# A two-layer decoder trunk: the norms' factors moved from ScalarE and VectorE to a power on GpSimd

## The chip, the cores and the metric

The kernel runs on one core of a Trainium2 chip. A core has a matrix engine (PE), with its weight loads shown apart (PEld), a vector engine (DVE), a scalar engine (ACT) and GpSimd (POOL). Each executes its own queue in order, and they meet at semaphores. DMA transfers are issued from the queues of SyncE (SP), ACT and POOL. The metric is the device time of one launch in microseconds; lower is better. A time given for a kernel is the median of several runs, and beside it stands one profiled execution, whose trace is read.

## The reference

The input x has 1024 rows of 1024 floats, the memory mem has 256 rows of 1024. Two layers follow one another, and everything is in float32:

```python
def rmsnorm(x, g):
    y = x * lax.rsqrt(jnp.mean(x * x, axis=-1, keepdims=True) + EPS)   # EPS = 1e-6
    return y * g

mem_n = rmsnorm(mem, mem_norm_g)
for i in range(2):
    hn = rmsnorm(x, attn_norm_g[i])
    mix, q_cross = mla_mixer(hn, ...) if i == 0 else swa_mixer(hn, ...)
    cross = memory_cross_attention(q_cross, mem_n, w_mem_kv[i])
    x = x + jnp.concatenate([mix, cross], -1) @ w_o[i]
    x = x + squared_relu_mlp(rmsnorm(x, mlp_norm_g[i]), w_up[i], w_down[i])
return rmsnorm(x, final_norm_g)
```

Layer 0's mixer is multi-head latent attention (12 heads, causal over all rows); inside it two more norms act on the low-rank query part (384 columns) and key-value part (256 columns). Layer 1's mixer is a sliding window of 128 with sinks. The MLP is `relu(h @ w_up)**2 @ w_down`, with 4096 hidden columns.

What the change touches is the factor of each norm, one number for each row: `1 / sqrt(mean(x*x) + EPS)`.

## The kernel before, in words

**Tiling.** Rows lie on the 128 partitions, so x is eight tiles of 128 rows and mem two; a norm's factor is one number in each partition, a 128x1 operand. Matrix products are done in a split of float32 into two parts: ACT copies the rounded part (L99 and L102, the names end in h), DVE subtracts to get the rest (L100 and L103, names in l), and PE does three products for one. So every operand of PE goes through ACT and then DVE. A normed row tile must also be transposed by PE before it can be an operand.

**Order of the work.** The program is written through a framework that takes the program's operations, estimates when each could run, and lays down one in-order queue for each engine, so an instruction's place in its queue depends on what the framework expects of all the others. Nobody wrote the order of the queues by hand, but it is fixed when the kernel is built.

**Stages**, with the times in the profiled execution:
- Head, to 62 us. The memory arrives, is transposed (psTm, L473), split (memTh, memTl) and multiplied by the memory weights (psmk, L342 to L344; the weight's parts are wmh and wml). The first tiles of x are scaled by their factors (fa, L209), transposed (psT_a, L216), split (xhls) and multiplied by the input weights wih and wil (psin). DVE computes the tables of the rotary embedding there too (rt, L244 to L293). The copies ktok and mrs belong to the memory's keys: mrs is the factor of a memory tile.
- Layer 0's inputs and attention, to about 500 us.
- Output projection of layer 0 (`wo_phase`, pswo), about 480 to 540 us: each of eight row tiles is added to x (L1294), written to DRAM by two DMAs from POOL's queue (L1303), normed (L1225 to L1231) and transposed (psT_m, L1241; called T_m(0) to T_m(7) here, by their places in the order). The first products of the MLP (psu, psv, L1421 to L1423) stand behind them in PE's queue.
- MLP of layer 0. The products are arranged as a seven-product scheme of block matrices, so that operands are sums and differences that DVE makes. The down projection (class `Down`, psy and psz, L1728 to L1730) adds its result to x (L1681), writes it out from POOL's queue (L1699), norms it (L1700 to L1710) and transposes it (psT_b, L1721; T_b(0) to T_b(7)) for layer 1.
- Layer 1 likewise; its down projection ends with the final norm, whose rows are scaled (L1707, L1712) and written out from the queues of SP and ACT.

**The norms.** There are 50 factors to compute, in two forms.

`rstd_of` (L172 to L181) with `newton` (L183 to L193) serves 18: the two memory tiles (`mem_root`, L477 on), the eight tiles of x (`norm_y`, L206), and the eight tiles in `a_in` (L618), where the query and key-value parts are done together as two columns. ACT squares the row and accumulates the sum (L179), DVE forms mean plus epsilon (L180), ACT takes the root (L187), DVE the reciprocal (L188) and one correcting Newton step (L189 to L192).

The class `Rstd` (L1141 to L1160) serves the other 32: eight in each output projection and eight in each down projection. Squares are accumulated for two halves of a row (`half`, L1150), already scaled to a mean; `get` adds the halves and epsilon on DVE (L1154), takes the root on ACT (L1155), the reciprocal on DVE (L1156), and the correcting step on DVE (L1157 to L1159). Its scratch columns lie in tiles named cosb and sinb, so these names mark the steps in the trace.

A root on ACT needs its function table: where another function ran before, a table load precedes it. At the start one small activation (L518) makes ACT load the table for the root early.

## Time and profile before

| | |
|---|---|
| median of three runs | 2112.05 us (2109.84 to 2112.26) |
| the profiled execution, its own time | 2109.36 us |
| span, first to last instruction | 2107.5 us |
| busy: PE, PEld | 2082.1 us (99%), 1691.0 us (80%) |
| busy: DVE, ACT, POOL | 1476.6 us (70%), 1114.6 us (53%), 147.9 us (7%) |
| mean granted clock of the matrix engine | 0.999 |
| DMA | 292.34 MB, mean 139 GB/s |

How to read it: busy time is the time in which an engine executed something; a matmul's end is modelled, and matmuls are pipelined, so an almost full PE is one that hardly ever lacked an operand. Rows of the timeline give the start, the duration, the engine, the source line, the operation, output and input names and the shape; a bracket at the end gives how long the engine had stood before, and what released it. In the list of waits a row reads: who waited, for whom, and the total, the count and the longest. Line numbers are those of the kernel before, unless said otherwise.

### The profile page before, as it was taken

The numbers are of one execution on the slowest core, as the hardware profiler recorded it, in microseconds if no ns is written. First come the engines' busy times: TensorE is split into PE (matmuls) and PEld (weight loads), VectorE is DVE, ScalarE is ACT, GpSimd is POOL, SyncE is SP. The second block draws the span as 40 slices with busy tenths as digits, with TensorE's granted clock in tenths as the row PEclk, the third lists the DMA queues.
The fourth block names the chain that finished last, engine by engine and source line by source line (L and its number), as shares of the span: only waits on it lengthen the run. The fifth ranks groups of instructions, "written<-read, shape, count | busy, mean of one in ns | idle before, by whom it ended". The sixth has DMA issues, their size and how long they took to land.

```text
span 2107.5 us, 28961 instructions
## 1 busy us (share of the span) xinstructions
PE 2082.1 (99%) x9830; PEld 1691.0 (80%) x9830; DVE 1476.6 (70%) x2929; ACT 1114.6 (53%) x2408; POOL 147.9 (7%) x248
## 2 busy tenths in 40 slices
PE   8999999999999999999999999999999999999998
PEld 7888766678888888888888878778788888888887
DVE  8766677775977776976557535666977776976565
ACT  7554466656755444444445435776755444444453
POOL 1001001010000000000001133420000000000000
PEclk9999999999999999999999999999999999999999
DMA  6202223343355446954433634542345446844342
GB/s 237 79 1 76 63 64 92 91 136 100 112 169 165 152 143 231 321 152 156 136 119 103 153 90 126 140 136 85 111 164 165 159 141 231 318 150 154 119 120 88
DMA packets 180756, 292.34 MB, mean 139 GB/s; under 512 B 16659, under 2 KB 70784, under 8 KB 180608
## 3 DMA queue, kind: packets, MB, share of 16 engines
q1 hardware_dynamic: 174096, 272.07, 41.4%
q0 software_dynamic: 5200, 15.80, 2.1%
q10 hardware_dynamic: 1312, 2.63, 0.4%
q8 instruction: 77, 1.26, 0.3%
q14 instruction: 71, 0.58, 0.1%
HBM read 187.34 MB, written 81.18 MB: 127 GB/s over the span
## 4 chain that ended last, share of the span: by engine, by line
PE 90%; DVE 5%; DMA 2%; ACT 2%; issue 1%; SPq 0%; DVEq 0%; ACTq 0%
PE psy L1730 5%; PE psy L1728 5%; PE psy L1729 5%; PE psu L1421 5%; PE psu L1422 5%; PE psu L1423 5%; PE psz L1728 4%; PE psz L1730 4%; PE psz L1729 4%; PE psv L1422 4%; PE psv L1421 4%; PE psv L1423 4%; PE pso L947 4%; PE pss L917 3%; PE pswo L108 3%; PE pswo L110 3%
## 5 line engine op out<-in xcount | busy, mean ns | idle before, releaser
L927 ACT ACTIVATE p<-pss 128x512 f32<-128x512 f32 (+2 forms) x144 | 68.7, 487 | 69.2 <-DVE pss L925 52.5
L1728 PE MATMUL psy<-g 128*128 128x512 f32 x256 | 99.9, 390 | 0.0
L1729 PE MATMUL psy<-g 128*128 128x512 f32 x256 | 99.6, 389 | 0.0
L1730 PE MATMUL psy<-g 128*128 128x512 f32 x256 | 99.4, 390 | 0.0
L99 ACT ACTIVATE g<-i 128x512 fp32r<-128x512 f32 x79 | 49.7, 629 | 92.5 <-PE psz L1729 46.0
L100 DVE TENSOR_TENSOR g<-i,g 128x512 fp32r<-128x512 f32 x79 | 55.6, 704 | 47.6 <-ACT g L99 47.6
L99 ACT ACTIVATE i<-mr 128x512 fp32r<-128x512 f32 x78 | 47.8, 628 | 74.0 <-PE psy L1729 25.6
L796 DVE TENSOR_REDUCE m<-psx 128x1 f32<-128x1024 f32 (+7 forms) x96 | 72.0, 752 | 20.1 <-PE psx L795 19.7
L99 ACT ACTIVATE uh<-i 128x512 fp32r<-128x512 f32 x66 | 41.7, 631 | 83.9 <-PE psy L1729 39.5
L947 PE MATMUL pso<-p,vf 128*128 128x512 f32 (+2 forms) x192 | 85.4, 527 | 0.6 <-ACT p L927 0.6
L100 DVE TENSOR_TENSOR uh<-i,uh 128x512 fp32r<-128x512 f32 x66 | 45.6, 690 | 46.8 <-ACT uh L99 46.6
L1728 PE MATMUL psz<-g 128*128 128x512 f32 x192 | 74.7, 389 | 0.0
L1729 PE MATMUL psz<-g 128*128 128x512 f32 x192 | 74.7, 389 | 0.0
L1730 PE MATMUL psz<-g 128*128 128x512 f32 x192 | 74.7, 389 | 0.0
L1320 ACT ACTIVATE mr<-mr,gcol 128x256 f32<-128x256 f32 (+1 forms) x160 | 63.9, 475 | 13.5 <-DMA mr<-in_mlp_w_up_dram 13.5
L100 DVE TENSOR_TENSOR i<-mr,i 128x512 fp32r<-128x512 f32 x78 | 53.6, 687 | 21.5 <-ACT i L99 21.5
L917 PE MATMUL pss<-qh,kh 97*128 97x512 f32 (+2 forms) x144 | 67.9, 474 | 0.0
L917 PE MATMUL pss<-ql,kh 97*128 97x512 f32 (+2 forms) x144 | 58.2, 404 | 0.0
L1641 DVE TENSOR_TENSOR mqf<-mqq,mqf 128x512 f32<-128x512 f32 x64 | 43.4, 688 | 20.6 <-DMA mqq<-in_mlp_w_down_dram 20.3
L1730 PEld LDWEIGHTS psy<-g 128*128 128x128 f32 x256 | 48.1, 188 | 10.0
L1729 PEld LDWEIGHTS psy<-g 128*128 128x128 f32 x256 | 48.1, 188 | 9.9
L1728 PEld LDWEIGHTS psy<-g 128*128 128x128 f32 x256 | 48.1, 188 | 9.8
(658 smaller groups left out, 6862.2 us busy)
## 6 DMA issues: line engine op xcount, KB each, us to landing
i<-hd SPq DMA_DIRECT2D x154, 256.0 KB
hd<-uh SPq DMA_DIRECT2D x76, 256.0 KB
hd<-ul SPq DMA_DIRECT2D x76, 256.0 KB
mr<-in_mlp_w_up_dram SPq DMA_DIRECT2D x36, 512.0 KB
hd<-x SPq DMA_DIRECT2D x72, 256.0 KB
mr<-hd SPq DMA_DIRECT2D x70, 256.0 KB
d<-in_mlp_w_up_dram SPq DMA_DIRECT2D x32, 512.0 KB
mqq<-in_mlp_w_down_dram SPq DMA_DIRECT2D x32, 512.0 KB
```

The source lines that it names most:

```text
L99: nc.scalar.activation(hi, src, AF.Copy)
L100: nc.vector.tensor_tensor(lo, src, f32(hi), ALU.subtract)
L796: nc.vector.reduce_max(m8s[h][:, i : i + 1], ps[:, :n], axis=AX, negate=True)
L917: return lambda: nc.tensor.matmul(o, a, b, skip_group_check=True, **kw)
L927: nc.scalar.activation(p[:, c0:], ps, AF.Exp, scale=SC)
L947: mms.append(lambda: nc.tensor.matmul(o, a, b, skip_group_check=True, **kw))
L1421: nc.tensor.matmul(ps, wh[:, k, :], xh[:, k, :], start=p in (1, 2, 5) and k == 0, stop=False, skip_group_check=True)
L1422: nc.tensor.matmul(ps, wh[:, k, :], xl[:, k, :], start=False, stop=False, skip_group_check=True)
L1423: nc.tensor.matmul(ps, wl[:, k, :], xh[:, k, :], start=False, stop=k == 3, skip_group_check=True)
L1728: nc.tensor.matmul(ps, ah[:, j, :], bh, start=p in (1, 5, 2) and k == 0, stop=False, skip_group_check=True)
L1729: nc.tensor.matmul(ps, ah[:, j, :], bl, start=False, stop=False, skip_group_check=True)
L1730: nc.tensor.matmul(ps, al[:, j, :], bh, start=False, stop=k == NP - 1, skip_group_check=True)
```

## The change

Every factor is now one power: (mean of squares + epsilon) to the power −0.5, on POOL. In `rstd_of` the square's scale is the root of 1/n, so that ACT's accumulator holds the mean; POOL adds epsilon and raises to the power. In `get` POOL adds the halves and epsilon and raises to the power. The exponent is a pair of columns filled with −0.5 once at the start. The root, the reciprocal, the Newton steps and the scratch tiles zs are gone, and so is a function that nothing called (`rstd_halves`). The early small activation now asks for a sine, so the table loaded first is another.

```diff
     def rstd_of(pl, src_parts, junk):
...
-        z = pl.tile([P, 2], F32, tag="zs", bufs=4, name=f"zs{small_ct[0]}")
+        rs = pl.tile([P, 2], F32, tag="rs", bufs=4, name=f"rs{small_ct[0]}")
         for i, (ap, n) in enumerate(src_parts):
-            nc.scalar.activation(junk[:, :n], ap, AF.Square, accum_out=ss[:, i : i + 1])
-            nc.vector.tensor_scalar(z[:, i : i + 1], ss[:, i : i + 1], 1.0 / n, EPS, ALU.mult, ALU.add)
-        return newton(pl, ss, z[:, :k], k)
...
+            nc.scalar.activation(junk[:, :n], ap, AF.Square, scale=float(np.float32(n ** -0.5)), accum_out=ss[:, i : i + 1])
+        nc.gpsimd.tensor_scalar(ss[:, :k], ss[:, :k], EPS, None, ALU.add)
+        nc.gpsimd.tensor_tensor(rs[:, :k], ss[:, :k], neg_half[:, :k], ALU.pow)
         return rs
...
     nc.gpsimd.memset(padl, 0.0)
     nc.gpsimd.memset(padr, 0.0)
+    neg_half = padl[:, 32:34]
+    nc.gpsimd.memset(neg_half, -0.5)
...
-    nc.scalar.activation(padl[:, 0:1], eps_t, AF.Sqrt)
+    nc.scalar.activation(padl[:, 0:1], eps_t, AF.Sin)
...
         def get(self):
-            ss, z, rk, t = self.st[:, 0:2], self.st[:, 2:3], self.st[:, 3:4], self.st[:, 4:5]
-            nc.vector.tensor_scalar(z, ss[:, 0:1], ss[:, 1:2], EPS, ALU.add, ALU.add)
-            nc.scalar.activation(t, z, AF.Sqrt)
-            nc.vector.reciprocal(rk, t)
-            nc.vector.scalar_tensor_tensor(t, rk, z, rk, ALU.mult, ALU.mult)
-            nc.vector.tensor_scalar(t, t, -0.5, 1.5, ALU.mult, ALU.add)
-            nc.vector.tensor_tensor(rk, rk, t, ALU.mult)
+            ss, z, rk = self.st[:, 0:2], self.st[:, 2:3], self.st[:, 3:4]
+            nc.gpsimd.tensor_scalar(z, ss[:, 0:1], ss[:, 1:2], EPS, ALU.add, ALU.add)
+            nc.gpsimd.tensor_tensor(rk, z, neg_half[:, 0:1], ALU.pow)
             return rk
```

ACT's queue now holds two table loads in place of seven. Since the framework orders the queues anew, work around the norms moves too. The change's own lines are numbered lower by then: L1154 to L1159 became L1134 and L1135, L180 and L181 are the two POOL steps of `rstd_of`, and L209, L350, L480, L1699, L1721 and L1728 to L1730 are now L187, L330, L460, L1675, L1697 and L1704 to L1706.

The first place is DVE's queue at the very start. There ss, zs and rs are the first memory tile's sum, mean and factor, memTl the rest part of the transposed memory, gcol the gains. Before:

```order
L180 TENSOR_SCALAR zs_233<-ss_232 128x1
L188 RECIPROCAL rs_236<-ss_232 128x1
L189 TENSOR_TENSOR ss_232<-rs_236 128x1
L190 TENSOR_TENSOR ss_232<-ss_232,zs_233 128x1
L191 TENSOR_SCALAR ss_232<-ss_232 128x1
L192 TENSOR_TENSOR rs_236<-rs_236,ss_232 128x1
L480 COPY mrs_231<-rs_236 128x1
L131 COPY identb<-ident 128x128
L100 TENSOR_TENSOR memTl<-psTm_0_121,memTh 128x4x128
L166 COPY gcol<-psg_135 128x8
L100 TENSOR_TENSOR memTl<-psTm_4_128,memTh 128x4x128
```

After:

```order
L131 COPY identb<-ident 128x128
L100 TENSOR_TENSOR memTl<-psTm_0_122,memTh 128x4x128
L166 COPY gcol<-psg_136 128x8
L460 COPY mrs_232<-rs_234 128x1
L100 TENSOR_TENSOR memTl<-psTm_4_129,memTh 128x4x128
```

The norm's steps have left the queue, and the copy of the factor now stands between the two splits of the memory and takes its input from POOL.

The second place is DVE's queue some twenty instructions on, at 23 to 31 us of the profiled execution: the scaling of x's first two tiles (fa), splits of the memory weights (wml) and of the input weights (wil). Before:

```order
L192 TENSOR_TENSOR rs_291<-rs_291,ss_287 128x1
L209 TENSOR_SCALAR fa_86<-fa_86,rs_291 128x1024
L103 TENSOR_SCALAR wil<-fa_87,gcol,wih 128x928
L350 TENSOR_SCALAR ktok_0_300<-psmk_155,mrs_231 128x256
L188 RECIPROCAL rs_334<-ss_330 128x1
L103 TENSOR_SCALAR wil<-fa_87,gcol,wih 128x928
L350 TENSOR_SCALAR ktok_1_303<-psmk_155,mrs_244 128x256
L189 TENSOR_TENSOR ss_330<-rs_334 128x1
L103 TENSOR_SCALAR wml_2_350<-wm_102,gcol,wmh_2_349 128x512
L190 TENSOR_TENSOR ss_330<-ss_330,zs_331 128x1
L103 TENSOR_SCALAR wil<-fa_87,gcol,wih 128x928
```

After:

```order
L187 TENSOR_SCALAR fa_87<-fa_87,rs_277 128x1024
L103 TENSOR_SCALAR wml_1_296<-wm_103,gcol,wmh_1_295 128x512
L187 TENSOR_SCALAR fa_87<-fa_87,rs_314 128x1024
L103 TENSOR_SCALAR wml_2_327<-wm_103,gcol,wmh_2_326 128x512
L330 TENSOR_SCALAR ktok_0_283<-psmk_156,mrs_232 128x256
L103 TENSOR_SCALAR wil<-fa_88,gcol,wih 128x928
L330 TENSOR_SCALAR ktok_1_286<-psmk_156,mrs_239 128x256
L103 TENSOR_SCALAR wil<-fa_88,gcol,wih 128x928
L103 TENSOR_SCALAR wml_2_327<-wm_103,gcol,wmh_2_326 128x512
L103 TENSOR_SCALAR wml_3_365<-wm_103,gcol,wmh_3_364 128x512 x2
L251 COPY rt_434<-pos_i 128x8
```

The second fa and the wml have moved ahead of most of the wil, and the steps of the rotary table (rt), which stood behind all eight wil before, now come in groups between the second and the fifth of them.

The third place is the end of layer 0's down projection, on PE and POOL. PE before, where psy is the product and psT_b the transposition of a normed row tile:

```order
L1728 MATMUL psy_0_7974<-g_0_166_8001 128x512
L1729 MATMUL psy_0_7974<-g_0_166_8001 128x512
L1721 MATMUL psT_b_0_10155<-ident,d_0_157_7971 128x128 x4
L1721 MATMUL psT_b_1_10162<-ident,d_0_157_7971 128x128 x4
L1730 MATMUL psy_0_7974<-g_0_166_8001 128x512
L1728 MATMUL psy_1_7975<-g_0_164_7991 128x512
```

PE after:

```order
L1704 MATMUL psy_0_7827<-g_0_164_7844 128x512
L1705 MATMUL psy_0_7827<-g_0_164_7844 128x512
L1697 MATMUL psT_b_0_9984<-ident,d_0_157_7824 128x128 x4
L1697 MATMUL psT_b_1_9991<-ident,d_0_157_7824 128x128 x4
L1706 MATMUL psy_0_7827<-g_0_164_7844 128x512
L1704 MATMUL psy_0_7827<-g_0_165_7849 128x512
```

Each of the last two products has nine matmuls; T_b(4) stood behind eight of the first of them, and now stands behind two. The transposition that follows it, T_b(5), stood behind the last product, and now stands ahead of it. POOL after, whose DMAs write the row to DRAM (before, the four DMAs stood there alone):

```order
L1675 DMA x_4680<-d_0_154_7821 128x512
L1134 TENSOR_SCALAR sinb<-sinb 128x1
L1135 TENSOR_TENSOR sinb<-sinb,padl 128x1
L1675 DMA x_4680<-i_0_155_7822 128x512
L1134 TENSOR_SCALAR cosb<-cosb 128x1
L1135 TENSOR_TENSOR cosb<-cosb,padl 128x1
L1675 DMA x_4680<-d_0_154_7821 128x512
```

Each norm's two steps now alternate with the DMAs. In the output projections they alternate with those of L1303 in the same way, and there PE's queue has moved too: between T_m(6) and T_m(7) stood 22 matmuls of the MLP in layer 0 and 24 in layer 1, and now 12 stand there in each.

18 lines of the change are left out of this document (removed).

## The prediction

> **What bounds the kernel now.** I read the page first: span, busy shares, chain.
>
> ```profile
> span 2107.5 us, 28961 instructions
> PE 2082.1 (99%) x9830; PEld 1691.0 (80%) x9830; DVE 1476.6 (70%) x2929; ACT 1114.6 (53%) x2408; POOL 147.9 (7%) x248
> PE 90%; DVE 5%; DMA 2%; ACT 2%; issue 1%; SPq 0%; DVEq 0%; ACTq 0%
> ```
>
> PE is busy for 2082.1 of 2107.5 us, so all that a change off PE can win is inside the 25.4 us in which PE stands. The page with the time beside this trace gives 2109.36 us: 1.86 around the span, 2.69 under the median of 2112.05.
>
> Next the windows (start:end, length, then PE, PEld, DVE, ACT, POOL busy with counts, granted clock, DMA share, GB/s), to see in which stage PE stands and who is full there.
>
> ```profile
> 0.00:20.00 20.00, 15.13 (x59) 12.00 (x60) 12.10 (x32) 13.08 (x24) 7.09 (x32) 1.00 0.94 329
> 20.00:35.00 15.00, 13.24 (x68) 10.56 (x66) 13.52 (x30) 14.19 (x23) 0.00 (x0) 1.00 0.87 304
> 50.00:62.00 12.00, 11.11 (x61) 9.07 (x59) 11.86 (x65) 5.16 (x14) 0.07 (x1) 1.00 0.31 97
> 520.00:560.00 40.00, 39.39 (x191) 32.31 (x190) 37.47 (x80) 33.38 (x71) 2.17 (x4) 1.00 0.23 74
> 2060.00:2107.50 47.50, 39.88 (x176) 32.69 (x175) 23.31 (x64) 14.71 (x39) 0.00 (x0) 0.97 0.24 89
> ```
>
> PE stands for 4.87 us in the first 20, 1.76 in 20 to 35, 0.89 in 50 to 62, 0.61 in 520 to 560, 7.62 at the end. In 20 to 35 DVE (13.52) and ACT (14.19 of 15) are nearly full, in 50 to 62 DVE alone (11.86 of 12). Then PE's waits, and who ended them:
>
> ```profile
> PE psTm L473 <- DMA mem<-in_mem_dram: 4.6, 1, 4.6
> PE psmk L343 <- DVE wml L103: 1.8, 2, 1.3
> PE psT_m L1241 <- ACT d L1230: 0.8, 2, 0.6
> PE psT_a L216 <- DVE fa L209: 0.6, 1, 0.6
> ```
>
> The first is the input's load, out of reach; in the others small steps of a norm stand in DVE's queue.
>
> **The change, part by part.** Each of the 50 norms loses ACT's Sqrt and four to six DVE steps, and gains two POOL instructions (add epsilon, power). DVE loses 276 instructions: 26 of L180, 18 times five of L188 to L192, 32 times five of L1154 to L1159; POOL gains 100 and a memset. Prices:
>
> ```profile
> L1967 POOL COPY sp<-sinks_b 128x3 f32<-128x3 f32 x32 | 5.8, 190 | 22.2 <-PE pswt L2006 22.2
> L312 POOL TENSOR_TENSOR fa<-fa 128x16 f32<-128x16 f32 x8 | 1.8, 223 | 113.8 <-DVE fa L309 106.8 <-ACT qc L372 7.0
> L147 POOL TENSOR_SCALAR sinks_b<-sinks_b 128x12 f32<-128x12 f32 x1 | 0.5, 525 | 5.2 <-DMA sinks_b<-in_swa_sinks_dram 5.2
> L1841 POOL TENSOR_TENSOR wsr<-wsr,gcol 128x1024 f32<-128x1024 f32 x12 | 22.9, 1905 | 346.9 <-DMA wsr<-in_swa_w_in_dram 301.8 <-DVE fb L103 25.7 <-DVE g L100 19.4
> ```
>
> No power is in this trace. The add I take at 0.20 (nearest: 190 and 223 ns). The power is one element a partition like the small copy, but a costlier function than L312's arithmetic on 16: 0.30, between 0.19 and the 1.90 of L1841, the longest kind with that shape of operands. The ends are far apart; by size it is nearest to the short ones. I call p the power's time.
>
> *The tail.* The last norm has no cover:
>
> ```profile
> 2100.64 0.63 ACT L1150 ACTIVATE i<-i 128x512 f32<-128x512 f32 x1 [2.59 <-DVE i L1681]
> 2101.18 0.19 ACT L1150 ACTIVATION_READ_ACCUMULATOR i<-i 128x1 f32 x1
> 2101.40 0.21 DVE L1154 TENSOR_SCALAR cosb<-cosb 128x1 f32<-128x1 f32 x1 [0.79 <-ACT i L1150]
> ...
> 2102.72 0.75 DVE L1712 SCALAR_TENSOR_TENSOR i<-i,cosb,mr 128x512 f32<-128x512 f32 x1
> ```
>
> From L1154 to L1712 it takes 1.32 us. After: 0.20 + p + two hand-overs of 0.05 (ACT's accumulator at 2101.37 to DVE at 2101.40 is 0.03) = 0.60 with p = 0.30. So −0.7; zero at p = 1.0, +0.9 at 1.9. POOL issues nothing here (0.00 in the last window), and is free.
>
> *The head.* The order puts the first norm's steps behind the first split of the memory:
>
> ```profile
> 5.72 0.15 DVE L180 TENSOR_SCALAR zs<-ss 128x1 f32<-128x1 f32 x1 [5.72 <-ACT fa L179]
> 7.32 0.68 DVE L100 TENSOR_TENSOR memTl<-psTm,memTh 128x512 fp32r<-128x512 f32 x1
> 8.05 1.11 PE L473 MATMUL psTm<-ident,mem 128*128 128x128 f32 x4 [0.22 <-DVE memTl L100]
> ```
>
> That split need no longer queue behind six norm steps, and PE's 0.22 goes: −0.2. What is left of that norm on DVE, a copy, now waits for POOL's power with the second split behind it: add 5.75, a mask memset, power to about 6.5, copy due at about 7.4. It costs nothing up to p = 1.2.
>
> *20 to 62 us.* PE's waits there:
>
> ```profile
> 30.11 0.14 DVE L192 TENSOR_TENSOR rs<-rs,ss 128x1 f32<-128x1 f32 x1
> 30.18 0.73 DVE L103 SCALAR_TENSOR_TENSOR wml<-wm,gcol,wmh 128x512 fp32r<-128x512 f32 x1
> 30.97 0.49 PE L343 MATMUL psmk<-wml,memTh 128*128 128x512 f32 x1 [1.28 <-DVE wml L103]
> 55.98 0.75 DVE L209 TENSOR_SCALAR fa<-fa,rs 128x1024 f32<-128x1024 f32 x1
> 56.78 1.09 PE L216 MATMUL psT_a<-ident,fa 128*128 128x128 f32 x8 [0.65 <-DVE fa L209]
> ```
>
> The new order takes DVE's weight splits wml ahead of two pieces of wil (1.1 us each), and the fa that PE waited for at 56.78 ahead of most of the rope table. The second wml, the one at 30.18, then has ahead of it from 21.7 us on: two other wml and two fa (0.67 each from start to start), two small copies (0.4), two wil (1.1), and with its own 0.73 it is done at 28.1, or 28.6 if DVE stands half a microsecond for the second fa's power. PE without its 1.76 of waits asks for it at 30.97 − 1.76 = 29.2. So the 1.76 may go whole, and the 0.65 too, −2.4 at best. Against it stand the table steps that now precede three pieces of wil (some 1.3 us), and ACT, which at 14.19 of 15 gets no emptier than three Sqrts at 0.2. I take −1.5, between −2.4 and +1.5 (the table steps in full on PE's path, and no wait gone).
>
> *From output projection to MLP, both layers.* T_m is the transposition of the normed row:
>
> ```profile
> 534.20 0.21 DVE L1154 TENSOR_SCALAR cosb<-cosb 128x1 f32<-128x1 f32 x1
> 538.32 0.48 DVE L1231 TENSOR_SCALAR d<-i,cosb 128x512 f32<-128x512 f32 x1
> 539.49 0.77 PE L1241 MATMUL psT_m<-ident,d 128*128 128x128 f32 x5 [0.61 <-ACT d L1230]
> ```
>
> The steps from L1154 to L1159 are spread over 4.1 us, each queued behind some bigger job of DVE; on POOL they are not. T_m(6) loses its wait, 0.6 in layer 0 and 0.2 in layer 1. But T_m(7) now follows 12 matmuls after T_m(6), where it followed 22 and 24: 12 at 0.23 is 2.7 us, and with the transposition itself (0.77 and more) some 3.5, for the sum of the row, Square (0.63 + 0.19), POOL (0.6), and scaling (0.48) in busy queues of ACT and DVE. I charge 0.2 a layer: −0.4. Past p = 0.7 each further microsecond falls on PE twice.
>
> *End of layer 0's down projection.* Here POOL also issues DMAs:
>
> ```profile
> 1150.42 0.57 POOL L1699 DMA_DIRECT2D x<-d  x1 [31.20 <-DVE d L1681]
> 1150.70 0.19 ACT L1150 ACTIVATION_READ_ACCUMULATOR d<-d 128x1 f32 x1
> 1152.72 0.92 DVE L1710 TENSOR_SCALAR d<-d,sinb 128x512 f32<-128x512 f32 x2
> 1153.39 1.06 PE L1721 MATMUL psT_b<-ident,d 128*128 128x128 f32 x8
> ```
>
> The add starts at 1150.99, behind the DMA, and with 0.2 + p + 0.05 the scaling at about 1151.6, done by 1152.5 (0.92 for both halves). The new order wants T_b(4) six matmuls earlier, 1153.39 − 6 × 0.23 = 1152.0. PE waits 0.5: +0.5, and one for one with p. T_b(5) moves ahead too, by nine matmuls, to 1152.5 + 1.06 + 7 × 0.23 = 1155.2; its row's DMA ends on POOL at about 1153.0, so add, power and scaling are done by 1154.6, in time.
>
> *At nothing.* The other 40 or so norms run under PE matmuls: PE's list of waits has no row for psT_b, two instances for psT_m and one for psT_a, so all other normed rows come in time today, and a chain of 0.6 in place of 1.3 to 4.1 us does not make them late. In the output projection POOL issues DMAs too, each as long as the 0.57 us above, but ACT's Square and accumulator (0.73 from start to end) start with it and last longer. What would uncover them is p above some 1.5 us. The table loads of ACT go:
>
> ```profile
> 496.45 1.28 ACT L1155 ACT_TABLE_LOAD   x1
> 497.74 0.20 ACT L1155 ACTIVATE cosb<-cosb 128x1 f32<-128x1 f32 x1
> ```
>
> Without Sqrt five of the seven loads leave, 6.4 us of ACT at 1.28 each; no wait of PE in the list has one behind it. The Trainium skill ("ScalarE: Activation LUTs", What ACT_TABLE_LOAD costs) adds about 1.38 us of drain to each switch, so 13.3 us of ACT by it. The Sqrt behind the load at 496.45 starts 1.29 us after it, so the trace shows no drain; on PE's path neither sum lands.
>
> The sum: −0.7 − 0.2 − 1.5 − 0.4 + 0.5 = −2.3, rounded with the up to 0.9 more that the 20 to 62 us stretch may give to −3: 2106.4 in the trace's own terms, 2109.0 against the median.
>
> **The rivals.**
>
> *Slow power (the other side).* If p is 1.9, as L1841, the tail gives +0.9, the head +0.7 (its copy holds the second split), T_m(7) +1.2 twice, T_b(4) +2.1, and the stretch to 62 us, where both fa wait for a power, some +1.6 instead of −1.5: +7.7, about 2120. It decides from p = 1.0 on. For it: L147 took 525 ns on 12 columns where L312 took 223 on 16, so POOL's price goes by the operation and not by size alone. Against: no POOL row of few columns passes 0.53.
>
> *First power slow only.* L147, the first of its kind, took 525 ns on 12 columns, so the first power may start late; the head absorbs 0.9 of it, then DVE's second split and PE wait one for one. At 6 us lost in the head it ends at about 2114. The Trainium skill ("GPSIMD Engine Reference", Instruction dispatch) has a first call to a freshly loaded kernel pay about 6 us; that would be this case, and no row here shows it.
>
> *Held-up DVE.*
>
> ```profile
> L1159 DVE TENSOR_TENSOR sinb<-sinb x16: 149/159/1858, 503.8 to 2086.2; 128x1 f32<-128x1 f32 x16
> 1113.56 1.89 POOL L1841 TENSOR_TENSOR wsr<-wsr,gcol 128x1024 f32<-128x1024 f32 x1 [2.71 <-DMA wsr<-in_swa_w_in_dram]
> ```
>
> One L1159 of 16 took 1858 ns, beside POOL's 1.89. If each of 100 POOL steps holds DVE for its own 0.25 us, DVE loses 25 us, about half of what leaves it (276 at some 0.17); only the full stretch to 62 us feels it, some 2 us: 2111.
>
> *All waits go.* With the table steps harmless and T_m(7), T_b(4) in time: −0.7 − 0.6 − 2.4 − 0.8 = −4.5, 2107.5, about the edge of a measurable gain.
>
> *No change at all* (the power is done on DVE anyhow): excluded, the instructions name POOL.
>
> **How the numbers follow.** Forecast 0.45 (2107.9 to 2111); all waits go 0.23 (2105 to 2107.8); held-up DVE 0.09 (2111); slow power 0.14 (2114 at p = 1.2 to 2120); first power 0.05 (2114); an order that costs PE in the first 62 us 0.04 (2116.5). 0.2%, 4.2 us, is what a measurement of this kernel can tell: under 2107.8 faster, over 2116.3 slower. The forecast is faster in a fifth of its cases, all waits go nearly always: 0.32; slow power, bad order and a share for runs that sit at either end of the shown 2109.84 to 2112.26: slower 0.2; same 0.48. The range 2104.5 to 2118 leaves out the worst of the slow power and gains larger than any wait listed.
>
> **What would show it.** A power row under 0.4 us on POOL; L1712's last instance about 0.6 us after its Square's accumulator; no PE wait at 28, 31 and 57 us; PE's wait at T_m(7) and T_b(4) under 1 us; five table loads fewer; PE's busy sum unchanged. The prediction falls if the power takes over 1 us, or if PE's new waits come from wil or xhls before 62 us.

## The result and the profile after

| | before | after |
|---|---|---|
| median | 2112.05 us (2109.84 to 2112.26) | 2119.52 us (2118.86 to 2122.83) |
| ratio, 95% interval | | 1.0044 [1.0033, 1.0055] |
| profiled execution, its span | 2109.36, 2107.5 us | 2119.09, 2117.4 us |

The changed kernel is slower by 7.5 us between the medians; the ratio beside them, 1.0044, is worth 9.3 us. The forecast was 2109.0 with a range to 2118.0, so the kernel ended outside it, on the slow side. The first lines of the page of the changed kernel:

```profile
span 2117.4 us, 28794 instructions
PE 2083.5 (98%) x9830; PEld 1693.9 (80%) x9830; DVE 1439.3 (68%) x2653; ACT 1100.7 (52%) x2353; POOL 200.9 (9%) x349
```

The change does what it says. DVE has 276 instructions fewer and 37.3 us less work, ACT 55 fewer (50 roots and five table loads) and 13.9 us less, POOL 101 more and 53.0 us more. PE's work grew by 1.4 us only. But PE stands for 33.9 us of the span where it stood for 25.4: 51 us were taken from DVE and ACT, and PE waits 8.5 us more.

The windows of the changed kernel (columns as in the prediction) show in which stages:

```profile
20.00:35.00 15.00, 15.00 (x74) 12.56 (x73) 11.54 (x32) 11.31 (x18) 2.10 (x4) 1.00 0.79 277
35.00:50.00 15.00, 12.32 (x67) 10.60 (x66) 14.68 (x33) 11.05 (x19) 1.56 (x2) 1.00 0.29 91
50.00:62.00 12.00, 11.73 (x64) 10.37 (x61) 11.08 (x41) 4.56 (x14) 1.92 (x4) 1.00 0.37 136
520.00:560.00 40.00, 37.69 (x180) 31.32 (x179) 32.50 (x54) 31.29 (x64) 6.72 (x12) 0.96 0.21 71
...
2060.00:2117.40 57.40, 47.69 (x211) 39.18 (x209) 23.98 (x37) 17.70 (x41) 10.77 (x16) 0.94 0.23 84
```

and one window of the kernel before that the prediction did not show:

```profile
35.00:50.00 15.00, 15.00 (x75) 13.14 (x74) 14.39 (x47) 10.39 (x21) 0.00 (x0) 1.00 0.13 54
```

From 20 to 35 us PE no longer stands (1.76 before), but from 35 to 50 it stands for 2.68 (0 before). From 520 to 560 it stands for 2.31 (0.61), at a mean granted clock of 0.96 (1.00). PE's waits in the changed kernel say for what:

```profile
PE psT_m L1217 <- ACT d L1206: 4.4, 2, 2.3
PE pskm L339 <- DVE ktok L330: 1.5, 1, 1.5
...
PE pscT L401 <- DVE cps L441: 1.1, 2, 0.9
PE pskm L339 <- DVE xhls L100: 1.1, 1, 1.1
...
PE psT_b L1697 <- DVE i L1686: 0.9, 1, 0.9
PE psT_b L1697 <- DVE d L1686: 0.9, 1, 0.9
```

L1217 is the transposition T_m (L1241 before), L1697 is T_b, L1206 and L1207 are the scalings ahead of T_m, L1270 is the add of the projection's result. T_m(7) waits 2.31 us in layer 0 and 2.04 in layer 1, T_b(4) and T_b(5) some 0.9 each.

**What a power costs.** The groups by line of the changed kernel (shortest, median and longest in ns, then the first and the last start in us):

```profile
L181 POOL TENSOR_TENSOR rs<-ss,padl x18: 538/620/805, 6.2 to 133.4; 128x1 f32<-128x1 f32 x10, 128x2 f32<-128x2 f32 x8
L1135 POOL TENSOR_TENSOR cosb<-cosb,padl x16: 559/562/576, 499.0 to 2109.7; 128x1 f32<-128x1 f32 x16
L1134 POOL TENSOR_SCALAR sinb<-sinb x16: 291/302/3698, 504.2 to 2093.0; 128x1 f32<-128x1 f32 x16
```

The power is 0.56 us where 0.30 was taken, the add 0.30 where 0.20 was taken. Some adds took longer, one of them 3.70; more on that below.

**T_m(7) in layer 0**, in the timeline of the changed kernel. The first four rows are row tile 6's add, its power and its scaling, the others belong to row tile 7:

```profile
537.16 1.07 POOL L1134 TENSOR_SCALAR cosb<-cosb 128x1 f32<-128x1 f32 x1
...
538.31 0.56 POOL L1135 TENSOR_TENSOR cosb<-cosb,padl 128x1 f32<-128x1 f32 x1
...
538.90 0.72 ACT L1206 ACTIVATE d<-i,cosb 128x512 f32<-128x512 f32 x1 [1.47 <-POOL cosb L1135]
538.90 0.49 DVE L1207 TENSOR_SCALAR d<-i,cosb 128x512 f32<-128x512 f32 x1 [0.77 <-POOL cosb L1135]
...
542.30 0.69 DVE L100 TENSOR_TENSOR g<-x,g 128x512 fp32r<-128x512 f32 x1 [0.82 <-ACT g L99]
...
542.91 0.69 DVE L1270 TENSOR_TENSOR i<-pswo,i 128x512 f32<-128x512 f32 x1
...
545.05 0.56 POOL L1135 TENSOR_TENSOR cosb<-cosb,padl 128x1 f32<-128x1 f32 x1
...
545.64 0.72 ACT L1206 ACTIVATE d<-i,cosb 128x512 f32<-128x512 f32 x1 [0.76 <-POOL cosb L1135]
...
546.42 1.71 PE L1217 MATMUL psT_m<-ident,d 128*128 128x128 f32 x8 [2.31 <-ACT d L1206]
...
547.78 0.78 PE L1397 MATMUL psv<-mqq,uh 128*128 128x512 f32 x1
```

Row 6's add took 1.07 us in place of 0.30, beside two instructions of DVE (536.84 to 538.14; 1.06 in layer 1). From the end of ACT's accumulator (536.92) to the scaling the factor took 1.98 us. ACT stood for 1.47 us and DVE for 0.77 until POOL had it. Both queues are in order, so all that stood behind the two scalings came later: splits of operands and four gains of weights on ACT, and on DVE the split of g that waits for ACT's. The add of row 7 (L1270) stands behind that split and began at 542.91, though its projection had ended on PE at 540.46. So row 7 was late before its own norm began, and then its add (0.37) and power (0.56) followed. PE stood for 2.31 us, and after that it was granted less than its clock:

```profile
541.00:550.00 9.00, 6.69 (x29) 5.41 (x27) 7.33 (x13) 8.24 (x18) 1.54 (x3) 0.82 0.08 32
```

By the trace's record of the clock this is a stretch of 3.41 us at 0.50, from 546.74 to 550.15, or 1.7 us of lost work. In layer 1 T_m(7) waited 2.04 us, and the clock stayed at 1.00.

**The end**, first as the chain that ended last in the changed kernel (start, duration, engine and line), then rows of its timeline:

```profile
2107.73 0.70 DVE i L1657
2108.50 0.49 issue
2109.62 0.61 POOLq L2120
2110.25 0.75 DVE i L1688
```

```profile
2109.28 0.30 POOL L1134 TENSOR_SCALAR cosb<-cosb 128x1 f32<-128x1 f32 x1 [4.50 <-ACT i L1130]
2109.66 0.56 POOL L1135 TENSOR_TENSOR cosb<-cosb,padl 128x1 f32<-128x1 f32 x1
...
2110.25 0.75 DVE L1688 SCALAR_TENSOR_TENSOR i<-i,cosb,mr 128x512 f32<-128x512 f32 x1 [1.83 <-POOL cosb L1135]
...
2111.00 0.33 SPq L1684 DMA_DIRECT2D out_dram<-i  x1
```

From the down projection's add (2107.73) to the last scaling (2110.25) it takes 2.52 us, where it took 2.80. But from the issue of the last output DMA to the end of the span it now takes 6.4 us (2111.00 to 2117.4), where it took 4.0 (2103.51 to 2107.5). The row `POOLq L2120` is the start of a closing instruction in POOL's queue, a drain, which the trace has from 2109.62 to 2116.60: it begins about where POOL's last work does and ends 6.4 us after that work is over. The kernel before has the same drain, 6.93 us long, at 1486.36, where POOL's last work lay and nobody waited for it.

### The profile page after: what moved, and what is told of

Read it like the earlier page. It is cut to its first block, busy times and chain, and to the rows that moved or that the text cites. A ratio compares the mean times of both kernels' runs of the same rounds, so it can differ in the third digit from the quotient of the medians.

```text
span 2117.4 us, 28794 instructions
## 1 busy us (share of the span) xinstructions
PE 2083.5 (98%) x9830; PEld 1693.9 (80%) x9830; DVE 1439.3 (68%) x2653; ACT 1100.7 (52%) x2353; POOL 200.9 (9%) x349
## 4 chain that ended last, share of the span: by engine, by line
PE 69%; DVE 3%; DMA 1%; issue 1%; ACT 1%; POOL 1%; POOLq 0%; DVEq 0%; ACTq 0%
PE psy L1704 5%; PE psy L1706 5%; PE psy L1705 5%; PE psu L1397 5%; PE psu L1398 5%; PE psu L1399 5%; PE psz L1706 4%; PE psz L1705 4%; PE psz L1704 4%; PE psv L1398 4%; PE psv L1397 4%; PE psv L1399 4%; PE psf L108 2%; PE psf L110 2%; PE psf L109 2%; PE pswo L108 1%
## 5 line engine op out<-in xcount | busy, mean ns | idle before, releaser
L1704 PE MATMUL psy<-g 128*128 128x512 f32 x256 | 100.0, 391 | 0.0
L1706 PE MATMUL psy<-g 128*128 128x512 f32 x256 | 99.4, 390 | 0.0
L1704 PE MATMUL psz<-g 128*128 128x512 f32 x192 | 74.7, 389 | 0.0
L1706 PE MATMUL psz<-g 128*128 128x512 f32 x192 | 74.7, 389 | 0.0
L1134 POOL TENSOR_SCALAR sinb<-sinb 128x1 f32<-128x1 f32 x16 | 10.5, 657 | 598.6 <-ACT d L1130 586.8
L1706 PEld LDWEIGHTS psy<-g 128*128 128x128 f32 x256 | 48.1, 188 | 10.0
L1705 PEld LDWEIGHTS psy<-g 128*128 128x128 f32 x256 | 48.1, 188 | 9.9
```

Source lines behind the costliest of these rows:

```text
L1704: nc.tensor.matmul(ps, ah[:, j, :], bh, start=p in (1, 5, 2) and k == 0, stop=False, skip_group_check=True)
L1705: nc.tensor.matmul(ps, ah[:, j, :], bl, start=False, stop=False, skip_group_check=True)
L1706: nc.tensor.matmul(ps, al[:, j, :], bh, start=False, stop=k == NP - 1, skip_group_check=True)
```

## The experiments

Medians are compared with the kernel before on the same chip: 2110.55 for e1 to e4. e5 to e12 ran on another chip, all on the same one, where the kernel before took 2110.55 beside e5 to e8 and 2110.85 beside e9 to e12. Since PE's products hardly change their order, each kernel's trace can also be laid against that of the kernel before: the same matmul's start in both, subtracted, gives how much later it comes, and the growth of this from one place to the next is what a stage lost (us, worked out from starts in the timelines; the last column is the difference of the spans).

| | to 130 | to 446 | T_m, layer 0 (to 570) | to 1116 | T_b (to 1485) | T_m, layer 1 (to 1582) | to 2099 | end | span |
|---|---|---|---|---|---|---|---|---|---|
| after | 0.8 | 1.2 | 3.1 | −0.6 | 1.8 | 1.6 | −0.2 | 2.1 | 9.9 |
| e1 one copy of POOL last | 0.2 | 0.3 | 1.5 | 0.1 | 0.1 | 0.0 | −0.6 | 2.6 | 4.0 |
| e2 final norm old | 3.5 | 1.0 | 4.5 | 0.9 | 1.8 | 2.2 | −0.6 | 0.1 | 13.5 |
| e3 T_m(7), T_b late | 0.1 | 1.2 | 3.7 | 0.1 | −0.2 | 1.8 | 0.0 | 2.1 | 8.8 |
| e4 cheap operation | −0.3 | 0.7 | 0.4 | −0.1 | 1.0 | 1.1 | −0.2 | 1.7 | 4.3 |
| e5 `rstd_of` alone | 1.4 | 1.6 | 0.0 | −0.1 | 0.0 | −0.1 | −0.4 | 0.1 | 2.6 |
| e6 `Rstd` alone | 1.9 | 0.2 | 2.8 | 0.7 | 1.8 | 1.6 | 0.1 | 2.1 | 11.1 |
| e7 adds of two tensors | 0.8 | 1.1 | 2.7 | 0.0 | 2.0 | 2.4 | 0.0 | 2.2 | 11.2 |
| e8 output projections old | 0.2 | 1.1 | −0.1 | 0.2 | 1.8 | 0.0 | 0.2 | 2.1 | 5.5 |
| e9 three parts undone | 1.4 | 1.3 | 0.3 | −0.2 | −0.2 | −0.1 | 0.1 | 0.1 | 2.7 |
| e10 layer 0's down norms alone | 0.5 | 0.1 | −0.1 | −0.1 | −0.3 | −0.1 | 0.4 | 0.1 | 0.6 |
| e11 as e9, two rows old | 3.6 | 1.4 | 0.5 | 0.9 | −0.3 | 0.2 | 0.1 | 0.1 | 6.4 |
| e12 the change again | 0.9 | 1.3 | 4.2 | 0.5 | 1.8 | 2.1 | −0.4 | 2.1 | 12.5 |

These are single executions. How far a stage scatters by itself is seen where a kernel's norms there are those of before: 1.9 for e6 up to 130 us, and 1.5 for e1 in layer 0's T_m stage.

A part of this scatter is PE's clock. At the start PE's matmuls take 0.63 us in place of 0.39 for a while, to 16 us in e10 and nowhere behind 9 us in e8. Ahead of the tail the traces' records of the granted clock have these stretches at 0.50, each of 3.41 us, which can cost up to 1.7 us:

| trace | half rate from (us) |
|---|---|
| after | 546.74 |
| e1 | 446.94 |
| e2 | 45.47, 451.65, 550.64, 1502.96 |
| e3 | 555.30 |
| e6 | 448.35 |
| e7 | 1497.73 |
| e11 | 44.42 |
| e12 | 42.42, 448.61, 547.59, 1499.91 |
| before, e4, e5, e8, e9, e10 | none |

Those from 446 to 452 us lie early in the output projection and count in the column of T_m, layer 0. The one of e1 comes behind PE waits of 0.29, 0.69 and 0.37 us; the kernel before has 0.30, 0.70 and 0.38 at the same place and kept its full clock. Of the ten waits of 2.04 to 2.89 us at T_m(7) (after, e2, e6, e7, e12), six were followed by half rate and four were not, the longest among these. So a stretch comes in one execution and not in another, and a stage's loss in one trace is not its price. If each in the column of T_m, layer 0, is taken at the 1.5 us of e1, an estimate, the changed kernel, e2, e6 and e12 lose 1.2 to 1.6 us there without them.

**e1: does POOL's last work cost time at the end?** The kernel before, with one small copy on POOL behind the last norm's factor, and nothing else.

```diff
                 rs = r.get()
+                if layer == 1 and t == 7:
+                    nc.gpsimd.tensor_copy(padr[:, 0:1], rs)
```

> The kernel before, with one copy of 128x1 added on GpSimd that reads the last row tile's factor; nothing waits for it, and no other instruction moves. Theory of the drain (GpSimd's closing drain takes about 7 us, counted from its last instruction, and the end of the program waits for it): the copy ends at about 2102.8 us of the trace, the drain at about 2109.3, the span is about 2110.0 in place of 2107.5, +2 to +2.5 us. Rival (the longer end of the changed kernel comes from its output transfers, or from the profile's noise): the span stays within 0.3 us of the kernel before.

Measured 2113.56 us, ratio 1.0014 [1.0005, 1.0024], 3.0 over the kernel before. The copy is off every chain:

```profile
2104.10 0.19 POOL L1706 COPY padr<-cosb 128x1 f32<-128x1 f32 x1 [615.18 <-DVE cosb L1159]
```

The drain begins with it (2104.08, 6.59 us), and the span ends 2.6 us later after the last matmul than before. So 0.19 us of POOL's work that nobody needs costs 2.6 us when it stands last. This is shown, in the trace and in the time. The other 1.4 us of the span's 4.0 are scatter, mostly the stretch at half rate from 446.94 us.

**e2: the end mended in the changed kernel.** The eight norms of the last down projection in their old form, which `old=True` selects.

```diff
-                rs = r.get()
+                rs = r.get(old=layer == 1)
```

> The changed kernel, with the eight norms of layer 1's down projection (the final norm) computed as before on DVE and ACT. Theory of the drain: GpSimd's last work is in layer 1's output projection, some 600 us before the end, so its drain is hidden; from the last output DMA's issue to the end 4.0 us in place of 6.4, and the chain ahead of it 0.3 longer (2.80 in place of 2.52 us): -2.1 us against the changed kernel, about 2117.4. Rival (the end is set by something else): no gain, or +0.3 us.

Measured 2119.71 us, 1.0046 [1.0031, 1.0061]. In the trace the drain lies at 1501.17 and the end loses 0.1 where it lost 2.1, as expected; the time does not show the gain. The same trace, the slowest of this kernel's four executions (2122.69 us), lost 3.5 us up to 130 us and 4.5 in the T_m stage of layer 0, in code that the edit does not touch, with three stretches at half rate in these two. The changed kernel itself loses 4.2 in that stage in another execution (e12), so most of this is scatter; that the mended end shows in the time is not shown by this run.

**e3: is it the order?** The transpositions that wait are moved behind other matmuls: T_m(7) behind the next group of products, T_b(4) and T_b(5) back to where their rows are ready.

```diff
+        go(1, 1, m.fill[1][1])
...
-        go(1, 1, m.fill[1][1])
...
+                            if layer == 0 and j in (1, 3):
+                                with tc.issue_after(last_mm[0]):
+                                    T(*late.pop(0))
...
-                                if j:
+                                if j == 3:
```

> The changed kernel, with PE's queue put back at three places by the order of the program alone: T_m(7) of both layers behind 24 matmuls of the MLP in place of 12, T_b(4) behind nine matmuls in place of two and T_b(5) behind the last nine. All norms stay on GpSimd. Theory of the order (the framework put these transpositions where their rows are not ready, and the power's own time matters little): PE's waits of 2.3 and 2.0 us at T_m(7) and 0.9 and 0.9 at T_b vanish, and so does the stretch of matmuls at half rate behind the first (1.5 us): -6 to -6.5 us against the changed kernel, about 2113. Theory of the price (GpSimd's steps of 0.3 and 0.56 us are what is too long): the rows are late wherever they stand, waits of 1 us or more remain at three of the four places, -1 to -3 us.

Measured 2118.0 us, 1.0034 [1.0021, 1.0047]. At T_b the loss is gone (−0.2 in place of 1.8). At T_m(7) the wait is gone and the loss is not (3.7, with a stretch at half rate from 555.30 in it, and 1.8): PE waits there for other operands instead, as the list of waits of e3 shows.

```profile
PE psu L1398 <- DVE mqf L100: 2.5, 2, 1.2
...
PE psu L1397 <- ACT mqf L99: 1.7, 2, 1.5
```

These are splits of the MLP's own operands. So at T_b the order was the cause, and at T_m(7) it was not: whatever PE does next there comes late out of ACT and DVE.

**e4: the price of the power.** Power replaced by a product. The factors are then not those of a norm; every instruction, wait and place stays.

```diff
-        nc.gpsimd.tensor_tensor(rs[:, :k], ss[:, :k], neg_half[:, :k], ALU.pow)
+        nc.gpsimd.tensor_tensor(rs[:, :k], ss[:, :k], neg_half[:, :k], ALU.mult)
...
-            nc.gpsimd.tensor_tensor(rk, z, neg_half[:, 0:1], ALU.pow)
+            nc.gpsimd.tensor_tensor(rk, z, neg_half[:, 0:1], ALU.mult)
```

> The changed kernel, with the power replaced by a multiplication on GpSimd of the same operands (by 0.001 in place of an exponent of -0.5; the factors are not those of the norm). The order of every queue stays that of the changed kernel. Theory of the price: 0.2 us in place of 0.56 at each step takes 0.35 us off each wait at T_m(7) (twice), T_b(4), T_b(5) and the memory's and input's stages, and with the long wait shorter PE keeps its full rate behind T_m(7): -2 to -4 us, 2115.5 to 2117.5. Theory of the order: no more than the 0.35 us at each of four places, -1.4 us, about 2118, and the half rate behind T_m(7) stays.

Measured 2114.19 us, 1.0018 [1.0008, 1.0027], under the 2115.5 that was expected at the least. By the groups and waits of e4 the operation took 0.19 us, and T_m(7) waited half as long:

```profile
L1135 POOL TENSOR_TENSOR cosb<-cosb,padl x16: 189/190/192, 497.4 to 2104.4; 128x1 f32<-128x1 f32 x16
```

```profile
PE psT_m L1217 <- ACT d L1206: 2.1, 2, 1.2
```

With 0.37 us less for each factor T_m(7) of layer 0 waited 1.17 us in place of 2.31, PE's clock stayed full from 541 to 550 us, and the stage lost 0.4 in place of 3.1. This is more than the price itself: the powers of rows 6 and 7 both lie ahead of that wait, and no half rate followed it. One trace does not show that it never would. ACT still stood for 1.09 us (1.47), since row 6's add was as long as in the changed kernel (1.10). So even a power as cheap as a small copy leaves the kernel slower than before, by T_b, the T_m stage of layer 1 and the end.

**e5 and e6: one form alone.** In e5 only `rstd_of` is changed (18 norms, to 134 us), in e6 only the class `Rstd` (32 norms); the other form is that of before.

```diff
         def get(self):
-            nc.gpsimd.tensor_scalar(z, ss[:, 0:1], ss[:, 1:2], EPS, ALU.add, ALU.add)
-            nc.gpsimd.tensor_tensor(rk, z, neg_half[:, 0:1], ALU.pow)
+            nc.vector.tensor_scalar(z, ss[:, 0:1], ss[:, 1:2], EPS, ALU.add, ALU.add)
+            nc.scalar.activation(t, z, AF.Sqrt)
...
```

and for e6

```diff
     def rstd_of(pl, src_parts, junk):
...
-        nc.gpsimd.tensor_scalar(ss[:, :k], ss[:, :k], EPS, None, ALU.add)
-        nc.gpsimd.tensor_tensor(rs[:, :k], ss[:, :k], neg_half[:, :k], ALU.pow)
...
+        return newton(pl, ss, z[:, :k], k)
```

> The kernel before, with the change made in rstd_of alone (18 norms, all before 135 us); the 32 norms of the class Rstd stay on DVE and ACT. PE's queue has the changed kernel's order up to 200 us and the old one behind it. Theory (the loss is in the norms of Rstd and in the end): 0 to +2 us against the kernel before, which is what the changed kernel's trace shows at 205 us (+2.0, of it up to 1.1 from PE's slower start); GpSimd's drain is hidden. Rival (the head's new order costs most): +4 us or more.

> The kernel before, with the change made in the class Rstd alone (32 norms). The head has the old order. Theory (the loss is in the norms of Rstd and in the end): T_m(7) of layer 0 +3.1 with the matmuls at half rate behind it, T_b +1.8, T_m(7) of layer 1 +1.6, the drain +2.1, a gain of 0.5 in the MLP: about +8 us against the kernel before. Rival: +4 us or less.

e5 measured 2112.3 us, 1.0009 [0.9999, 1.0018]; e6 2118.39 us, 1.0035 [1.0023, 1.0047]. The two medians are 1.8 and 7.8 over the kernel before. The loss is in `Rstd`, at T_m, T_b and the end; the early norms bring no gain. That 7.8 meets the expected 8 is in part luck: in e6's trace T_m(7) of layer 0 waited 2.31 us and the half rate expected behind it did not come (granted clock 1.00 from 543 to 552 us), while another stretch, from 448.35, stands in that stage's 2.8.

**e7: does another form of add escape the long hold?** The add with scalar operands is replaced by adds of two tensors, one in `rstd_of`, two in `get`.

```diff
-            nc.gpsimd.tensor_scalar(z, ss[:, 0:1], ss[:, 1:2], EPS, ALU.add, ALU.add)
+            nc.gpsimd.tensor_tensor(z, ss[:, 0:1], ss[:, 1:2], ALU.add)
+            nc.gpsimd.tensor_tensor(z, z, eps2[:, 0:1], ALU.add)
```

> The changed kernel, with GpSimd's tensor-scalar addition replaced by additions of two tensors (one in rstd_of, two in get, epsilon from a column). Theory of the held addition (the tensor-scalar form stands while DVE runs back to back on operands in SBUF: 1.07, 1.06 and 3.70 us in place of 0.30 at T_m(6) of both layers and in the final norm): no addition over 0.3 us, the chain at T_m(6) 0.6 us shorter, -1 to -2 us against the changed kernel. Rival (whatever GpSimd starts under such a run of DVE is held): the first of the additions takes the same 1.07 and 3.7 us, and the time is the same or 0.5 us longer.

Measured 2121.57 us, 1.0052 [1.0035, 1.0069]. The timeline of e7, POOL only:

```profile
2067.48 0.62 POOL L1136 TENSOR_TENSOR sinb<-sinb 128x1 f32<-128x1 f32 x1 [0.57 <-ACT i L1132]
2068.17 2.99 POOL L1137 TENSOR_TENSOR sinb<-sinb,padl 128x1 f32<-128x1 f32 x1
```

The first add came through between two instructions of DVE, the second was held to the end of DVE's run. At T_m(6) the two adds took 0.54 and 0.52, together as long as the one add of 1.07. So the form does not free the add. With one more instruction in each chain T_m(7) waited 2.89 and 2.29 us (2.31 and 2.04), but the median, 11.0 over the kernel before, cannot be told from the changed kernel's own 10.4 on this chip (e12).

**e8: the output projections undone.** The 16 norms ahead of T_m in their old form, all else as changed.

```diff
-            rs = rst.pop(t).get()
+            rs = rst.pop(t).get(old=True)
```

> The changed kernel, with the 16 norms of the two output projections computed as before on DVE and ACT. PE's order at T_m(6) and T_m(7) is that of the kernel before, T_b and the final norm stay as changed. Theory (DVE and ACT stand in these norms for GpSimd's chain of DMA, addition and power, and the MLP's first operands queue behind them): the losses of 3.1 us in layer 0 and 1.6 us in layer 1 go, -4 to -5 us against the changed kernel, +3 to +4 against the kernel before. Rival (something else than these norms is late at the start of the MLP): -1 us or less.

Measured 2115.35 us, 1.0024 [1.0014, 1.0033]. The waits of e8:

```profile
PE psT_b L1706 <- DVE i L1695: 0.9, 1, 0.9
PE psT_b L1706 <- DVE d L1695: 0.9, 1, 0.9
...
PE psT_m L1226 <- ACT d L1215: 0.7, 2, 0.5
```

T_m waits for 0.7 us in all, as in the kernel before (0.8), and its stage loses nothing in either layer; T_b and the end stay as they were in the changed kernel. The median is 4.8 over the kernel before, where 3 to 4 were expected. PE's order at T_m(6) and T_m(7) is that of the kernel before again, so this run takes away the norms and the order together; e3, where T_m(7) stood behind 24 matmuls and the norms were still on POOL, shows that the order alone does not do it. The old form, with its six steps in DVE's and ACT's queues, is the better one there.

**e9: three parts undone together.** Old norms in the output projections (e8) and in the last down projection (e2), T_b late (e3). What is left on POOL are `rstd_of` and layer 0's down norms. Beside the lines on T_b of e3:

```diff
-            rs = rst.pop(t).get()
+            rs = rst.pop(t).get(old=p in range(8))
...
-                rs = r.get()
+                rs = r.get(old=layer == 1)
```

> The changed kernel with three places undone: the norms of both output projections and of the final norm as before on DVE and ACT, and T_b(4), T_b(5) of layer 0 put back behind their matmuls. The 18 norms of rstd_of and the eight of layer 0's down projection stay on GpSimd. If the losses named so far are all there is, they add up: what is left is the head of the run with rstd_of alone (+1.75 us), and layer 0's MLP and down projection, which gave -0.5 and -0.25 in the traces: +1.0 to +1.5 us against the kernel before. If something else is lost, +3 us or more.

Measured 2112.07 us, 1.0009 [0.9999, 1.0018]: 1.2 over the kernel before, in the expected 1.0 to 1.5. No stage behind 446 us loses more than 0.3. The three losses are separate, and together they are nearly all.

**e10: only layer 0's down norms on POOL**, with T_b late; `rstd_of` is old as well. It asks whether anything in the change gains. To the edits of e9 comes

```diff
-        nc.gpsimd.tensor_scalar(ss[:, :k], ss[:, :k], EPS, None, ALU.add)
-        nc.gpsimd.tensor_tensor(rs[:, :k], ss[:, :k], neg_half[:, :k], ALU.pow)
...
+        return newton(pl, ss, z[:, :k], k)
```

> The kernel before with the power on GpSimd in the eight norms of layer 0's down projection alone, and T_b(4), T_b(5) behind their matmuls. The only stage in which a trace showed a gain with the power: -0.25 to -0.7 us against the kernel before if the gain is the change's, 0 to +0.5 if it was scatter; neither is far outside what the runs can tell. Above +1.5 us there is a loss that no trace has shown yet.

Measured 2110.62 us, 1.0002 [0.9992, 1.0011]. There is no gain to be told, and the −0.6 that the changed kernel shows between 570 and 1116 us is not there (−0.1), and the changed kernel in another execution has +0.5 (e12): it was scatter.

**e11: which rows of the output projection?** As e9, but only rows 6 and 7 of each output projection have the old norm.

```diff
-            rs = rst.pop(t).get(old=p in range(8))
+            rs = rst.pop(t).get(old=p in (6, 7))
```

> As the run with three places undone, but in the output projections only the last two rows (T_m(6), T_m(7)) are on DVE and ACT as before, the first six on GpSimd; a table load for the root then comes at the sixth row, where ACT is busiest, and not at the first. Theory (only the last two rows of a projection have DVE and ACT standing in the way of the MLP): the same as that run, within 1 us, but for the 1.28 us of the table load. Rival (the first six rows lose too): +2 us or more against that run.

Measured 2113.93 us, 1.0014 [1.0005, 1.0023], 1.9 over e9 with intervals that overlap. In the trace the two T_m stages lose 0.5 and 0.2 (e9: 0.3 and −0.1), so in these traces the first six rows cost 0.5 us there at most. The rest of its longer span lies up to 130 us, with a stretch at half rate from 44.42, and between 570 and 1116, in code that it shares with e9. The run does not say more.

**e12: the changed kernel once more**, without an edit, on the chip of e9 to e11.

> The changed kernel itself, on the chip of these runs, so that they can be compared with it: +7 to +9 us against the kernel before, with losses at T_m(7) of both layers, T_b and in the drain, and a scatter of some 1.5 us in the first 20 us, where the matmuls go over from half to full rate at another time in each run.

Measured 2121.22 us, 1.0050 [1.0035, 1.0065], 10.4 over the kernel before on this chip, more than the 7 to 9 expected, with losses at the same places; half rate followed T_m(7) in both layers here. With it the medians on one chip can be taken down step by step: e12 is 10.4 over the kernel before, e8 4.8, e9 1.2, e10 −0.2. So the norms of the output projections, with the order that goes with them, cost 5.6 us, T_b and the end 3.6 (4.0 in the traces of e8 and e9), `rstd_of` 1.4, which is inside the intervals. No version is faster than the kernel before by what can be told.

## Why the prediction was wrong, point by point

The prediction's sum was −2.3 us; the trace has +9.9. The step that failed worst is the overlap at T_m(7): a chain of 0.6 us for a factor, covered but for 0.2 us a layer. The runs showed a chain of 1.98 us at row 6, for which ACT and DVE stand, and 4.7 us lost in the trace where −0.4 was forecast (5.6 in the medians, e12 less e8). Next is the tail, where POOL's closing drain had no term: +2.1 for −0.7. The other terms are smaller: up to 446 us +2.0 for −1.7, and T_b +1.8 for +0.5.

**The power's price.** It took p = 0.30 and 0.20 for the add; they are 0.56 and 0.30. The choice of the row failed: the power was put beside the short steps "by size", while what counted for the slow power rival (a price that goes by the operation) was right: the product on the same columns takes 0.19. That rival was said to decide from p = 1.0 on, and its time, 2120, is nearly the result's, but it was reached at 0.56, by other ways. e4 shows how much hung on p: with 0.37 us less for each factor the ratio falls from 1.0044 to 1.0018, some 5 us (3.8 by the medians, each against its own kernel before).

**T_m, −0.4 forecast, +4.7 measured** (3.1 and 1.6; e8 takes it away). T_m(6) lost its wait, as forecast. The prediction saw that T_m(7) had come close to T_m(6), and added up row 7's own chain, for which it charged 0.2 us a layer. It left out that a scaling which waits for POOL holds up ACT and DVE, and that the add of row 7 stands behind them. By its rows, the add at row 6, beside DVE's run, came 0.77 us late (1.07 for 0.30), and the power only 0.26 (0.56 for 0.30). The prediction also had no term for the clock, which takes about half of the 3.1 here and none of the 1.6. What stands behind a waiting instruction on its own queue was asked for T_b, and not here. That it is these two queues, and not T_m's place alone, is shown by e3 (the place moved, the loss stays); that they stand for the 1.47 and 0.77 us is read from the trace, and was not taken away by itself.

**T_b, +0.5 forecast, +1.8 measured.** T_b(4) went as the prediction had it, one for one with the prices: 0.5 and 0.36 more is 0.86, as measured. T_b(5) was forecast in time and waited 0.90: its row's DMA ended on POOL (1158.50 + 0.62) 1.8 us behind the start of T_b(4), where the prediction had 0.5. The timeline of the changed kernel:

```profile
1157.35 1.07 PE L1697 MATMUL psT_b<-ident,d 128*128 128x128 f32 x8 [0.86 <-DVE d L1686]
...
1158.50 0.62 POOL L1675 DMA_DIRECT2D x<-i  x1 [1.81 <-DVE i L1657]
...
1159.71 0.56 POOL L1135 TENSOR_TENSOR cosb<-cosb,padl 128x1 f32<-128x1 f32 x1
...
1160.94 1.06 PE L1697 MATMUL psT_b<-ident,i 128*128 128x128 f32 x8 [0.90 <-DVE i L1686]
```

Add and power come behind that DMA on POOL's queue. e3 and e9 take all of T_b's loss away by order alone.

**The tail, −0.7 forecast.** The chain was shortened by 0.28; with the true prices, 0.36 dearer, the prediction's own sum would have given 0.34. The +2.4 behind it was not forecast at all: "POOL issues nothing here, and is free" was right on POOL's load and wrong on what follows the last thing that POOL does. e1 shows it.

**20 to 62 us, −1.5 forecast, about 0 measured** (PE stands for 2.95 us there, 2.65 before). The three waits named went away as argued. In their place came waits of 1.15 us for xhls and 1.53 us for ktok between 35 and 50 us, where DVE is busy for 14.68 of 15. The prediction had named waits for xhls before 62 us as what would bring it down. Behind it 1.2 us are lost up to 446 us, whenever `rstd_of` is on POOL (0.7 to 1.6 in the kernels with it, 0.1 to 0.3 in e1, e6 and e10); in the changed kernel one of its waits is for cps, 0.9 us. What in the order makes that wait was not taken apart.

**The head, −0.2 forecast:** PE's wait for memTl is gone. The scatter up to 130 us, from −0.3 to 3.6 over these kernels, is larger than such a term.

**Right:** the first power is not slow, so that rival falls:

```profile
6.23 0.57 POOL L181 TENSOR_TENSOR rs<-ss,padl 128x1 f32<-128x1 f32 x1
```

The instruction counts were right, PE's work hardly changed, and the five table loads left ACT without a gain that any run shows.

**The held-up DVE rival did not come true; the other way round did.** Beside DVE's runs it is POOL's small steps that become longer here. The prediction's row of 1858 ns, a DVE step beside an instruction of POOL of 1.89 us in the kernel before, is not contradicted by this. The timeline of the changed kernel, POOL and DVE:

```profile
2066.36 3.70 POOL L1134 TENSOR_SCALAR sinb<-sinb 128x1 f32<-128x1 f32 x1 [0.71 <-ACT i L1130]
...
2069.29 0.68 DVE L100 TENSOR_TENSOR i<-mqf,i 128x512 fp32r<-128x512 f32 x1
...
2070.74 0.75 DVE L1688 SCALAR_TENSOR_TENSOR i<-g,sinb,mr 128x512 f32<-128x512 f32 x1 [0.76 <-POOL sinb L1135]
```

DVE ran without a gap from 2066.16 to 2069.97, and the add, 0.30 us elsewhere, ended at 2070.06. PE did not wait for that row.

**Two slips in its working.** In the rival "all waits go" the term of 0.6 has no row; with the head's 0.2 in its place the sum is −4.1. And a norm loses five to seven steps of DVE, not four to six, though the total of 276 is right. Neither moves the forecast.

## What to carry to other kernels

An instruction moved to an idle engine is not free when in-order engines wait for its result: count what stands behind each waiting instruction, up to the next thing that the bottleneck needs. A wait of the matrix engine may bring a stretch at half rate, in one execution and not in the next, so one trace's loss at such a wait is not its price. A step on GpSimd at the very end of a kernel costs more than its duration (2.6 us for a copy of 0.19 here), so the engine's last work belongs well before the end. A saving of work on engines that are 70% and 53% busy was worth nothing by itself here; the old steps, six short ones in queues that were moving anyway, cost the matrix engine less than one hand-over to a third engine and back.

## What the runs showed of the hardware that was not expected

- **POOL's closing drain** takes 6.6 to 7.0 us from POOL's last work on. When that work is the kernel's last, the end of the program comes 2.4 us later after the last output DMA's issue in the changed kernel and 2.6 us in e1; when it lies earlier, the drain costs nothing (the kernel before, e2, e9).
- **POOL waits for a gap in DVE's run.** An add of 0.30 us took up to 3.70 us beside a run of DVE instructions (1.07 at T_m(6)), and ended under 0.1 us after the run. The Trainium skill ("SBUF — State Buffer", Who interferes with whom) says that a DVE instruction with two inputs in SBUF contends with a GpSimd instruction that reads SBUF. The trace agrees, and it is POOL that is blocked; it was blocked here for up to six DVE instructions in a row, and in e7 it once came through between two.
- **The clock can halve for 3.41 us behind a short wait, and does not do so each time.** A PE wait of 2.31 us at T_m(7) was followed by a stretch at 0.50 in the changed kernel, e2 and e12, and by none in e6; one of 2.04 us by a stretch in e2 and e12, and by none in the changed kernel and e6; one of 2.89 us (e7) by none. The Trainium skill ("TensorE: Matmul & The Clock Gate", What's actually happening) puts the clock down after an idle window of about 3.4 us that runs freely, without regard to the kernel. The length at half rate agrees with one such window, and that the same wait has either outcome fits one that runs freely; but every wait that brought it about here was shorter than a window.
- **A power of one element in each partition** takes 0.56 us on POOL, a product of the same shape 0.19.
